# A mixer's values and output gates taken out of its scan, as block products in a stage ahead of it

## The chip, the cores and the metric

The kernel runs on one core of a Trainium2 chip. The metric is the time of one execution on the device in microseconds (us). Its engines are PE (matrix products), DVE (vector), ACT (scalar and function tables), POOL (general) and SP, which here only issues transfers (DMAs) between DRAM and the on-chip memory.

## The reference

One layer: an HGRN2 mixer over 2048 latent tokens of width 1024, behind 256 context tokens, then a gated convolutional feed-forward part (FFN). In short (cut, and for one direction d of two):

```python
q, zf_fwd, zf_bwd, v, g = jnp.split(h @ w_in, 5, axis=-1)        # 8 heads of 128 each
f = lb[d] + (1.0 - lb[d]) * sigmoid(zf)                          # k = 1 - f, q = silu(q)
o_l, _ = hgrn2_chunk_scan(q, k, v, log(f), state_of_context)     # forward and backward, summed
y = (rmsnorm(o_l, g_gain) * silu(g)) @ w_out
lat = lat + g1 * y
lat = lat + g2 * conv_ffn(modulate(rmsnorm(lat), sh2, sc2))
out = rmsnorm(lat, final_g)
```

h is the normalized and modulated input. The vectors g1, sh2, sc2, g2 come from w_ada and the condition.

## The kernel before

Tokens lie in 16 tiles of 128; four tiles are a *unit* (512 tokens), two units a half: g=0 is tiles 0 to 7, g=1 tiles 8 to 15. Every large product is made from three: each fp32 operand is split into a high and a low part (`split`: ACT copies the high part, line 79, DVE subtracts, line 80), and PE adds high x high, high x low and low x high. So a projection of one head and one type for one unit is 8 k-steps of 3 matmuls, 24 of 128x512 (`step`, lines 470 to 472).

`mixer_scan` goes through 16 heads: g=0 with h=0..7, then g=1 with h=0..7. In each it projects two gates (types 2, 1), the query (0), the value (3) and the output gate (4) for the two units of its half. In g=0 it also does gates and value of the context (128x256). The weights of a type are loaded raw (`load_w`, 512 KB) and split in both passes. Values come out transposed and are turned back by PE (line 638). All the small work of the scan (the running products of the gates on DVE, lines 546 and 585, `kd`, `qi`, `km`, `qm`, the `scores` of 32x32 blocks at line 673, masks at 689, their sum `at` at 690, states, outputs at 725 and 728) is placed between the projections by an agenda: each k-step is one *tick*, and `at(clock + n, f)` runs f that many ticks later. Engines work through their instructions in the order in which this program text issues them.

The tokens of the first half are made in the first head (`unit_tok`), those of the second in heads 2 to 5 of g=0 (`make_tok`, `put_tok`, by way of DRAM). The rest of the modulation (`ada_rest`, 32 DVE steps at line 785 and four small products) runs in heads 0 to 5 of g=1, the weighting of the output weights (`out_scaled`, line 812) in heads 2 to 5. Results go to DRAM (`stash`). The FFN already makes its up-projection in 2x2 blocks by seven products (lines 1113 to 1116): the weights of two column blocks and two halves of K are A11, A12, A21, A22, the tokens of two units B11, B12, B21, B22, and sums of them (S1 to S4 of weights, T1 to T4 of tokens) give four results from seven products instead of eight.

Of the kernel before, what the change touches and what calls it, by code (L numbers as in the profile page):

```python
# [11 lines left out]
F32 = mybir.dt.float32  # L12
# [33 lines left out]
def body(ctx, tc, a, out):  # L46
# [104 lines left out]
    Sf = hp.tile([128, NH, 128], F32, name="Sf", tag="Sf", bufs=1)  # L151
    Sb = hp.tile([128, NH, 128], F32, name="Sb", tag="Sb", bufs=1)


    lp = pool_(ch, "lp")
    c1 = ctx.enter_context(ExitStack())
    wp = pool_(c1, "wp", 4)
    hq = pool_(c1, "hq")
    fix = pool_(c1, "fix")
    gp = pool_(c1, "gp", 2)  # L160
    xp = pool_(c1, "xp")
# [4 lines left out]
    TOK = [128, UT, 2, 4, 128]  # L166
    tok = {}
    tok_d = [[dr.tile(TOK, F32, name=f"tok{u}{kh}") for kh in range(2)] for u in range(2)]
    cxt = hq.tile([128, 2, 2, 2, 4, 128], F32R, name="cxt", tag="cxt", bufs=1)
# [6 lines left out]
    def put_tok(hm, t, kh):  # L176

        b = lp.tile([128, 2, 4, 128], F32R, name="stg", tag="stg", bufs=1)
        split(b[:, 0], b[:, 1], hm[:, 4 * kh:4 * kh + 4])
        sp.dma_start(tok_d[t // UT - 2][kh][:, t % UT], b.bitcast(F32))  # L180

    def x_tile(xt, t):
        src, r = (a["x"], t) if t >= 0 else (a["ctx"], t + 2)
        sp.dma_start(xt, src[r * 128:(r + 1) * 128])

    def load_w(h, ty):
        raw = rawp.tile([128, D], F32, name="raw", tag="raw")
        sp.dma_start(raw, a["w_in"][h, ty])
        w = wp.tile([128, 2, KT, 128], F32R, name="w", tag="w")
        split(w[:, 0], w[:, 1], raw.rearrange("p (k n) -> p k n", k=KT))  # L190
        return w

    def new_hm():
        return xp.tile([128, KT, 128], F32, name="hm", tag="hm", bufs=1)

    def load_x(xt, t, hm, *after):
        x_tile(xt, t)
        normalize(xt, hm.rearrange("p k n -> p (k n)"), gp, after)


    HEAD0 = (2, 1, 3, 0)
    staged = {}

    def stage(t):

        tag = ("ke", "ke", "qp", "qp", "qi", "qi", "xt", "hm", "stg", "raw")[t + 2]
        p = {"xt": xp, "hm": xp, "stg": lp, "raw": rawp}.get(tag, gp)
        staged[t] = p.tile([128, D], F32, name="x0", tag=tag, bufs=1 if p in (xp, lp) else 2)
        x_tile(staged[t], t)

    def turn_tok(tp, ts, ks):

        for i, k in enumerate(ks):
            for j, t in enumerate(ts):
                pe.transpose(tp[:, i, j], staged[t][:, k * 128:(k + 1) * 128], ident)
# [6 lines left out]
    with ExitStack() as c0:  # L222
        p0s = pool_(c0, "p0s", space=PSUM)
        silv = sil.rearrange("p (two k) -> p k two", two=2)
        silp = gp.tile([128, KT, 32], F32, name="silp", tag="kt", bufs=2)
# [5 lines left out]
        junk = lp.tile([128, D], F32, name="junk", tag="stg", bufs=1)  # L231
# [5 lines left out]
        def raw_w(ty):  # L237
            raw = rawp.tile([128, D], F32, name="raw", tag="raw")
            sp.dma_start(raw, a["w_in"][0, ty])
            return raw  # L240

        head0 = {}

        def split_head0(ty, raw):
            head0[ty] = w = wp.tile([128, 2, KT, 128], F32R, name="w", tag="w")
            return split(w[:, 0], w[:, 1], raw.rearrange("p (k n) -> p k n", k=KT))
# [10 lines left out]
        head_raw = {}  # L257
        for k in range(2, KT):
            ada_load(act, k, 0)
            ada_load(act if k >= KT - 2 else sp, k, 1)  # L260
            if k == KT - 3:
                head_raw[2] = raw_w(2)
        head_raw[1] = raw_w(1)
        for t in range(4):
            stage(t)
        for t in (-2, -1):
            norm_begin(staged[t], junk, gp)
        norm_end()
        late_junk = place(2, [128, D], F32, "junk")
# [6 lines left out]
        with tc.issue_after(squared[-1]):  # L276
            made = split_head0(2, head_raw[2])
        m2 = gp.tile([128, 512], F32, name="m2", tag="q", bufs=2)
# [15 lines left out]
        hmc = [gp.tile([128, 2, 2, 128], F32, name="hm", tag="gv"[g % 2], bufs=2) for g in range(4)]  # L294
# [4 lines left out]
        def split_ctx(g):  # L299
# [4 lines left out]
        order = [(evict_ctx, 1), (split_ctx, 0), (evict_ctx, 2), (split_ctx, 1), (split_head0, 1),  # L304
                 (evict_ctx, 3), (split_ctx, 2), (split_ctx, 3)]
        for f, g in order:
            with behind_of(made):
                made = f(g, head_raw[1]) if f is split_head0 else f(g)
        head_raw[3] = raw_w(3)
        head_raw[0] = raw_w(0)  # L310
        for t in range(4, 8):
            stage(t)
        with behind_of(made):
            for t in range(4):
                norm_begin(staged[t], late_junk, gp)
                if t == 1:
                    split_head0(3, head_raw[3])
            norm_end()


        l0, l1 = vec[:, V_LB:V_LB + 16], vec[:, V_LB + 16:V_LB + 32]
        lbw = gp.tile([128, 2, 128], F32, name="lbw", tag="so", bufs=2)
# [83 lines left out]

    def mixer_scan():
# [29 lines left out]
        Fs = [fix.tile([128, 2, NS, SEG], F32, name=f"F{i}") for i in range(2)]  # L437
        ABs = [fix.tile([128, UT, 128], F32, name=f"AB{d}") for d in range(2)]
        TBs = [fix.tile([128, 4, UT, 4], F32, name=f"TB{i}") for i in range(2)]
        TXs = [fix.tile([128, 2, UT, 4], F32, name=f"TX{i}") for i in range(2)]  # L440
        for i in range(2):
            pool.memset(Fs[i], 1.0)
            pool.memset(TBs[i], 1.0)
            pool.memset(TXs[i], 1.0)
            pool.memset(ABs[i], 0.0)


        clock = [0]
        agenda = []

        def at(when, f):
            heapq.heappush(agenda, (when, len(asked), f))
            asked.append(when)

        asked = []

        def run(until):
            while agenda and agenda[0][0] <= until:
                heapq.heappop(agenda)[2]()

        def tick():
            clock[0] += 1
            run(clock[0])

        stepped_pe = []

        def step(z, w, r, k):

            h, l = r[:, :, 0, k % 4], r[:, :, 1, k % 4]
            pe.matmul(z, w[:, 0, k], h, start=k == 0, stop=False, skip_group_check=True)  # L470
            pe.matmul(z, w[:, 0, k], l, start=False, stop=False, skip_group_check=True)  # L471
            stepped_pe[:] = [pe.matmul(z, w[:, 1, k], h, start=False, stop=k == KT - 1,  # L472
                                       skip_group_check=True).ins]
            tick()

        def acc(z, w, rs):

            for k in range(KT):
                step(z, w, rs[k // 4], k)
# [7 lines left out]
        evicted = {}  # L487

        def make_tok(t):

            got = []

            def load():
                got.append(xp.tile([128, D], F32, name="xt", tag="xt", bufs=1))
                got.append(new_hm())
                load_x(got[0], t, got[1], *((evicted["kt"], passed[-1]) if t % 2
# [1434 lines left out]
```

## Time and profile before

| | |
|---|---|
| three runs | 2728.62, 2728.97, 2731.67 us; median 2728.97 |
| span of the profiled execution | 2729.5 us (all that is shown of its time) |
| TensorE busy | 2698.7 us, 99% |
| VectorE, ScalarE, GpSimd busy | 1977.8, 1136.9, 572.9 us |
| mean DMA rate | 150 GB/s |

Busy time is the time in which an engine worked on something; with overlapping matmuls the mean length of one is longer than the step from one to the next. The window rows shown below have one stretch of time each, with busy time and count of each engine, then the granted clock of PE, the share of the DMA engines and the rate.

### The profile page before, as it was taken

The page shows a single profiled execution, that of the slowest core. Times are in us where ns is not written, and L with a number is a line of the kernel's source. Part 1 is how long each engine was busy: PE and PEld are TensorE (multiplying, and loading weights), DVE is VectorE, ACT ScalarE, POOL GpSimd, SP SyncE. Part 2 cuts the span into 40 slices and gives each one's busy share as a digit, 9 for nine tenths or more (in the row PEclk, how much of TensorE's full clock was granted, in tenths as well). Part 3 has the DMA queues.
Part 4 walks back from the last instruction along what each step waited for, and adds up shares of the span by engine and source line. Part 5 has one row for each costly group of instructions (what it writes and reads, how often), then busy time and mean ns, then how long its engine had stood idle before and what let it go on. Part 6 is the DMA issues. An engine that isn't in the chain of part 4 may idle for free.

```text
span 2729.5 us, 41987 instructions
## 1 busy us (share of the span) xinstructions
PE 2698.7 (99%) x16060; PEld 2252.7 (83%) x16060; DVE 1977.8 (72%) x2803; ACT 1136.9 (42%) x1887; POOL 572.9 (21%) x885
## 2 busy tenths in 40 slices
PE   7999999999999999999999999999999999999999
PEld 4888888888888888888888888888888888888887
DVE  4756655556767776668997888777877777578896
ACT  5334444323233233335666444444444444333444
POOL 3211111011111111211211543333434440000001
PEclk8999999999999999999999999999999999999999
DMA  6213323224544443228888232228322234988653
GB/s 240 86 53 105 106 83 97 86 87 163 167 124 137 149 137 113 87 80 297 300 300 344 93 93 82 73 79 307 93 76 79 78 93 137 309 279 289 200 185 131
DMA packets 229104, 410.56 MB, mean 150 GB/s; under 512 B 29604, under 2 KB 137508, under 8 KB 225064
## 3 DMA queue, kind: packets, MB, share of 16 engines
q1 hardware_dynamic: 224152, 398.65, 44.1%
q10 hardware_dynamic: 4752, 9.24, 0.9%
q8 instruction: 126, 2.06, 0.3%
q14 instruction: 74, 0.61, 0.1%
HBM read 293.23 MB, written 114.57 MB: 149 GB/s over the span
## 4 chain that ended last, share of the span: by engine, by line
PE 91%; DMA 3%; DVE 3%; ACT 1%; issue 1%; POOL 1%; SPq 0%; ACTq 0%; POOLq 0%; DVEq 0%
PE z L470 11%; PE z L472 11%; PE z L471 11%; PE y L1744 4%; PE y L1743 4%; PE y L1745 4%; PE zc L1113 3%; PE zc L1116 3%; PE zc L1115 3%; PE zd L1113 3%; PE zd L1115 3%; PE zd L1116 3%; PE za L1116 3%; PE za L1115 3%; PE za L1113 3%; PE kv L703 2%
## 5 line engine op out<-in xcount | busy, mean ns | idle before, releaser
L470 PE MATMUL z<-tok,w 128*128 128x512 f32 x1280 | 516.4, 404 | 0.0
L472 PE MATMUL z<-tok,w 128*128 128x512 f32 x1280 | 501.0, 391 | 0.0
L471 PE MATMUL z<-tok,w 128*128 128x512 f32 x1280 | 500.6, 391 | 0.0
L80 DVE TENSOR_TENSOR w<-raw,w 128x512 fp32r<-128x512 f32 (+1 forms) x258 | 237.2, 922 | 131.7 <-ACT w L79 127.8
L472 PEld LDWEIGHTS z<-tok,w 128*128 128x128 f32 x1280 | 240.4, 188 | 52.1
L470 PEld LDWEIGHTS z<-tok,w 128*128 128x128 f32 x1280 | 240.8, 188 | 45.7 <-issue 1.7
L471 PEld LDWEIGHTS z<-tok,w 128*128 128x128 f32 x1280 | 241.1, 188 | 43.9 <-DVE tok L80 0.2
L79 ACT ACTIVATE w<-raw 128x512 fp32r<-128x512 f32 (+1 forms) x258 | 194.8, 760 | 132.9 <-PE zd L1116 75.9
L1743 PE MATMUL y<-w,mh 128*128 128x512 f32 x600 | 233.4, 390 | 1.2 <-ACT X L1777 1.2
L1744 PE MATMUL y<-w,mh 128*128 128x512 f32 x600 | 233.6, 389 | 0.2 <-DVE w L80 0.2
L1745 PE MATMUL y<-w,ml 128*128 128x512 f32 x600 | 233.4, 389 | 0.0
L546 DVE TENSOR_TENSOR_SCAN S<-F,d 128x528 f32<-128x528 f32 (+1 forms) x80 | 91.3, 1144 | 119.1 <-ACT F L525 118.9
L80 DVE TENSOR_TENSOR w<-s,w 128x512 fp32r<-128x512 f32 x126 | 121.5, 967 | 57.2 <-ACT w L79 56.3
L75 POOL TENSOR_TENSOR rs<-rs,mhalf 128x1 f32<-128x1 f32 (+3 forms) x53 | 61.9, 1168 | 417.7 <-DVE rs L74 417.7
L79 ACT ACTIVATE w<-s 128x512 fp32r<-128x512 f32 x126 | 78.5, 628 | 150.5 <-POOL s L1181 83.5
L1113 PE MATMUL zc<-rT,w 128*128 128x512 f32 x352 | 137.1, 390 | 0.2 <-DMA rT<-rhs1T 0.2
L1116 PE MATMUL zc<-rT,w 128*128 128x512 f32 x352 | 136.9, 389 | 0.0
L1115 PE MATMUL zc<-rT,w 128*128 128x512 f32 x352 | 136.9, 389 | 0.0
L1743 PEld LDWEIGHTS y<-w,mh 128*128 128x128 f32 x600 | 112.6, 188 | 25.8 <-ACT X L1777 2.1
L1744 PEld LDWEIGHTS y<-w,mh 128*128 128x128 f32 x600 | 112.6, 188 | 23.9 <-DVE w L80 0.6
L1745 PEld LDWEIGHTS y<-w,ml 128*128 128x128 f32 x600 | 112.6, 188 | 23.3
L1116 PE MATMUL za<-rB,w 128*128 128x512 f32 x336 | 130.7, 389 | 0.0
(359 smaller groups left out, 6259.0 us busy)
## 6 DMA issues: line engine op xcount, KB each, us to landing
raw<-in_w_up_dram SPq DMA_DIRECT2D x88, 512.0 KB, 4.0
raw<-in_w_in_dram SPq DMA_DIRECT2D x80, 512.0 KB, 4.0
lr<-m SPq DMA_DIRECT2D x49, 512.0 KB, 5.2
m<-r SPq DMA_DIRECT2D x66, 256.0 KB, 4.3
spare<-in_w_ada_dram SPq DMA_DIRECT2D x32, 512.0 KB, 4.2
kq<-stash SPq DMA_DIRECT2D x15, 1024.0 KB, 8.0
og<-stash SPq DMA_DIRECT2D x30, 512.0 KB, 5.3
u<-in_w_down_dram SPq DMA_DIRECT2D x51, 256.0 KB, 3.5
```

The lines of the kernel that those rows point to most:

```text
L79: i = act.activation(h, src, AF.Copy)
L80: j = dve.tensor_tensor(l, src, h.bitcast(F32), OP.subtract)
L470: pe.matmul(z, w[:, 0, k], h, start=k == 0, stop=False, skip_group_check=True)
L471: pe.matmul(z, w[:, 0, k], l, start=False, stop=False, skip_group_check=True)
L472: stepped_pe[:] = [pe.matmul(z, w[:, 1, k], h, start=False, stop=k == KT - 1, skip_group_check=True).ins]
L546: dve.tensor_tensor_scan(flat(S[:, d]), flat(F[:, d]), flat(d1[:, 0:ns]), 0.0, OP.mult, OP.max)
L1113: pe.matmul(o, w[:, 0, k], r[:, :, 0, k], start=start and k == 0, stop=False, skip_group_check=True)
L1115: pe.matmul(o, w[:, 0, k], r[:, :, 1, k], start=False, stop=False, skip_group_check=True)
L1116: i = pe.matmul(o, w[:, 1, k], r[:, :, 0, k], start=False, stop=k == 3, skip_group_check=True)
L1743: pe.matmul(z, lh, rh, start=start, stop=False, skip_group_check=True)
L1744: pe.matmul(z, lh, rl, start=False, stop=False, skip_group_check=True)
L1745: pe.matmul(z, ll, rh, start=False, stop=stop, skip_group_check=True)
```

## The change

A stage `early()` stands ahead of the scan and makes all values, and the output gates of all heads in g=0 and of heads 0 to 5 in g=1. A `Heads` object is two heads of one type. With the tokens of the two units of a half they form the 2x2 blocks, and `product` runs one of the seven products, 4 k-steps of 3 matmuls. 105 products (15 pairs) stand in a list `todo`, and weights are prepared `LOOK` = 5 products ahead: raw load, sums S1 to S4 on POOL, splits on ACT and DVE. First come context values (`context_row`) while the tokens of g=1 are made (`unit0`, `unit1`, `differences`), then 7 pairs of g=1, then 8 pairs of g=0. During the first of these, `side_tokens` makes the factors of g=0, one tile of each unit at a time in four rounds, and sends them to DRAM (`tok_d`). When a product is the last of g=1 to use a factor, the factor's place is loaded with that of g=0 (2 MB). `ada_rest` now runs beside the g=0 products. Results are written by `finished`: gates after Silu to the stash, values after the turn (line 475) to `v_d`, context values to `cv_d`.

The scan keeps gates and queries. It loads v, splits weights in g=0 alone and stores them split (`w_d`, 1 MB each), to be loaded ready in g=1. `scores` and the three steps behind them stand 18, 20, 24 and 28 ticks behind a query's end; before they were 16 ticks behind the query, and 5, 9 and 13 behind the value of that unit. The output gates of heads 6 and 7 in g=1 stay plain, at the end of the last head. The context gates have F, TB and TX buffers of their own.

Core of the diff (the list of products, one product, the scan's head):

```diff
+        def multiply(z, w, r, start):
+            for k in range(4):
+                h, l = r[:, :, 0, k], r[:, :, 1, k]
+                pe.matmul(z, w[:, 0, k], h, ...)
+                pe.matmul(z, w[:, 0, k], l, ...)
+                pe.matmul(z, w[:, 1, k], h, ...)
+                tick()
...
+        for i in (0, 2):
+            todo += [(1, p, n) for n in ("B11", "B21") for p in vs[i:i + 2]]
+        for i in (0, 2):
+            todo += [(1, p, n) for n in FACTORS[2:] for p in vs[i:i + 2]]
+        gs = [Heads(4, h) for h in range(0, G_PLAIN, 2)]
+        todo += [(1, p, n) for n in FACTORS for p in gs[0:2]]
+        todo += [(1, gs[2], n) for n in ("B11", "T2", "B21", "T1", "T3", "B22", "T4")]
...
+            product(g, p, n)
+            if last_use[g, n] == i:
+                if g == 1:
+                    rhs[n] = factor_tile(n)
+                    sp.dma_start(rhs[n].bitcast(F32), tok_d[0][n])
...
             def query(u, after):
-                q = swish(project(weight(0), u), "q")
-                done = (made_tok[-1][1],) if first and u == 0 else ()
-                scores, made[u] = unit_steps(h, t0[u], factors(h, u, t0[u], q, done))
-                at(clock[0] + after, scores)
+                q = swish(project(weight(g, h, 0), u), "q")
+                v = values(v_d[h][t0[u] // UT])
+                for f, dt in zip(unit_steps(h, t0[u], factors(h, u, t0[u], q), v), after):
                     at(clock[0] + dt, f)
...
             gate(0)
-            query(0, 16)
+            query(0, (18, 20, 24, 28))
             gate(1)
...
-            value(0, (4, 7, 10) if last else (5, 9, 13))
...
-            out_gate(0)
-                value(1, (5, 9, 13))
-            out_gate(1)
```

ACT's order in the prologue, ahead of the first full products. Before, it is the split of context (`cxt`) and of weights, squares of the first unit (L107, for the norm) and the first gates:

```order
L79 ACTIVATE cxt_149<-hm_280 128x2x256
L107 ACTIVATE junk_213,ss_312<-x0_193 128x1024
L79 ACTIVATE w_323<-raw_300 128x1024
L107 ACTIVATE junk_213,ss_317<-x0_195 128x1024
L107 ACTIVATE junk_213,ss_326<-x0_197 128x1024
L107 ACTIVATE junk_213,ss_332<-x0_199 128x1024
L523 ACTIVATE F1_373<-z_390 128x8x32
L525 ACTIVATE F1_373<-F1_373,lb_111,oml_112 128x8x32
L523 ACTIVATE F1_373<-z_417 128x8x32
```

Now, from the first context values (L502) on, with squares of unit 1 (L129), the turned values (L476) and the weights of the third value pair (`w_541`, `w_544`):

```order
L502 ACTIVATE out_473<-zc_424 128x512
L129 ACTIVATE x0_229,ss_738<-x0_231 128x1024
L129 ACTIVATE x0_229,ss_744<-x0_231 128x1024
L476 ACTIVATE out_473<-tr_498 128x512
L129 ACTIVATE x0_229,ss_750<-x0_231 128x1024
L129 ACTIVATE x0_229,ss_756<-x0_231 128x1024
L502 ACTIVATE out_535<-zc_479 128x512
L476 ACTIVATE out_535<-tr_579 128x512
L79 ACTIVATE w_541<-raw_475 128x512
L79 ACTIVATE w_544<-raw_475 128x512
L79 ACTIVATE aside_384<-raw_477 128x512
```

The splits of that pair's weights stand behind four squares and the results of two context products.

SP's queue where the tokens of the next half come in. Before, that is at the end of g=0 (`tok`, four loads of 2 MB), between the scan's stores:

```order
L715 DMA stash_71<-qi 128x128
L1036 DMA tok<-tok_145 128x4096
L714 DMA stash_64<-sk 128x128
L714 DMA stash_65<-sk 128x128
L1036 DMA tok<-tok_146 128x4096
L748 DMA stash_64<-g 128x128
L748 DMA stash_65<-g 128x128
L748 DMA stash_66<-g 128x128
```

Now it is the turn from g=1 to g=0 in the new stage, with the factors `rB11`, `rT2`, `rB21`, `rT1` and the raw weights of the second value pair of g=0:

```order
L524 DMA stash11_75<-out_2173 128x128
L737 DMA rB11_2199<-tok0B11_131 128x4096
L737 DMA rT2_2218<-tok0T2_133 128x4096
L524 DMA stash8_72<-out_2241 128x128
L524 DMA stash9_73<-out_2241 128x128
L524 DMA stash10_74<-out_2241 128x128
L524 DMA stash11_75<-out_2241 128x128
L737 DMA rB21_2247<-tok0B21_132 128x4096
L583 DMA raw_1233<-in_w_in_dram 128x1024
L583 DMA raw_1233<-in_w_in_dram 128x1024
L737 DMA rT1_2273<-tok0T1_134 128x4096
```

Three of the 2 MB loads stand ahead of the two raw weights.

DVE in a head of g=1, from the next unit's scans to this unit's `at` (S and F are the running products, AB the masked scores, `spare` the weighted output weights). Before:

```order
L80 TENSOR_TENSOR w<-raw,w 128x1024
L546 SCALAR_TENSOR_TENSOR S<-F_373,d_369 128x528
L553 TENSOR_TENSOR ke<-S 128x512
L585 SCALAR_TENSOR_TENSOR F_373<-F_373,d_369 128x528
L546 SCALAR_TENSOR_TENSOR S<-F_373,d_369 128x528
L689 COPY_PREDICATED AB_374<-mb,sc_365 128x512
L689 COPY_PREDICATED AB_375<-mf,sc_366 128x512
L554 TENSOR_TENSOR ke<-S 128x16x32
L690 TENSOR_TENSOR at<-AB_374,AB_375 128x512
L785 SCALAR_TENSOR_TENSOR acc<-spare,sil,acc 128x1024
L585 SCALAR_TENSOR_TENSOR F_373<-F_373,d_369 128x528
```

Now:

```order
L938 TENSOR_TENSOR ke<-S 128x512
L970 SCALAR_TENSOR_TENSOR F_3697<-F_3697,d_3693 128x528
L931 SCALAR_TENSOR_TENSOR S<-F_3697,d_3693 128x528
L939 TENSOR_TENSOR ke<-S 128x16x32
L970 SCALAR_TENSOR_TENSOR F_3697<-F_3697,d_3693 128x528
L972 RECIPROCAL rt<-S 128x32
L957 TENSOR_TENSOR km<-ke,TX_3705 128x4x64
L1066 COPY_PREDICATED AB_3699<-mb,sc_3689 128x512
L1066 COPY_PREDICATED AB_3700<-mf,sc_3690 128x512
L957 TENSOR_TENSOR km<-ke,TX_3705 128x4x64
L1067 TENSOR_TENSOR at<-AB_3699,AB_3700 128x512
L1155 SCALAR_TENSOR_TENSOR spare<-spare,vec,g_9148 128x1024
L1083 SCALAR_TENSOR_TENSOR states<-Sf,sd,kv 128x128
```

The masks of a unit stand behind both scans of the next unit's second gate, its `rt` and half of its `km`; before they stood between them, and the projections of value and output gate lay behind the scores.

More of the change, by code (lines that the diff above doesn't have):

```diff
@@ L309, in body @@
[L309 to L317, printed above, removed]
-            norm_end()
+                made = f(g)
+        sp.dma_start(cxt_d, cxt.bitcast(F32))
+        p0.close()
+        ps = pool_(ce, "pse", 2, space=PSUM)
+        aside = place(2, [128, 4, 2, 4, 128], F32R, "aside")
@@ new lines, in early, with __init__, prepare @@
+        class Heads(Blocks):
+            def __init__(self, ty, h):
+                super().__init__(ring)
+                self.ty, self.h, self.z, self.loaded = ty, h, {}, False
+            def prepare(self, n):
+                if LEFT[n] in self.w:
+                    return
+                if not self.loaded:
+                    self.loaded = True
+                    self.raws([raw_tile() for _ in range(2)])
+                    for i, r in enumerate(self.raw):
+                        sp.dma_start(r.rearrange("p i k n -> p (i k n)"), a["w_in"][self.h + i, self.ty])
+                    self.sums(pool, *[pb.tile([128, 4, 128], F32, name=n, tag=n) for n in ("s1", "s2")])
+                self.split(LEFT[n])
@@ L739, in second @@
                 stepped(1)
-            return scores, (vs.append, lambda: stepped(0), second, lambda: outputs(1))
+            return scores, lambda: stepped(0), second, lambda: outputs(1)
         def keep_gate(h, t0, g):
```

810 lines of the change are left out of this document (506 added, 304 removed).

## The prediction

> **What bounds the kernel now.** I read the page's sums by engine and by chain first, then its costliest group, the time line of that group, and a table of windows by stage.
>
> ```profile
> span 2729.5 us, 41987 instructions
> PE 2698.7 (99%) x16060; PEld 2252.7 (83%) x16060; DVE 1977.8 (72%) x2803; ACT 1136.9 (42%) x1887; POOL 572.9 (21%) x885
> PE 91%; DMA 3%; DVE 3%; ACT 1%; issue 1%; POOL 1%; SPq 0%; ACTq 0%; POOLq 0%; DVEq 0%
> L470 PE MATMUL z<-tok,w 128*128 128x512 f32 x1280 | 516.4, 404 | 0.0
> ```
>
> PE is busy 99% of the span and carries 91% of the chain. L470 is one of three equal lines (L470, L471, L472), so the scan's projections are 3840 matmuls of 128x512. Their mean of 404 ns counts the overlap of one with the next; the time line has the real step:
>
> ```profile
> 567.73 0.39 PE L470 MATMUL z<-tok,w 128*128 128x512 f32 x1
> ...
> 574.99 0.39 PE L472 MATMUL z<-tok,w 128*128 128x512 f32 x1
> ```
>
> These are 33 rows, 32 steps in 7.26 us: 0.2269 us a matmul, each behind the last.
>
> ```profile
> core 0: us, PE busy (x) PEld busy (x) DVE busy (x) ACT busy (x) POOL busy (x), PEclk, DMA share, GB/s
> 0.00:35.00 35.00, 17.80 (x85) 4.22 (x85) 6.90 (x24) 7.82 (x13) 13.84 (x33) 0.90 0.96 378
> 35.00:102.00 67.00, 64.31 (x441) 54.51 (x442) 57.58 (x93) 41.99 (x72) 20.34 (x39) 0.95 0.21 75
> ...
> 557.00:635.00 78.00, 78.00 (x609) 67.36 (x608) 44.62 (x66) 24.11 (x42) 11.63 (x31) 1.00 0.29 89
> 635.00:702.50 67.50, 67.50 (x522) 57.16 (x521) 41.50 (x58) 20.25 (x34) 10.26 (x24) 1.00 0.62 210
> 702.50:772.00 69.50, 69.50 (x526) 57.26 (x525) 47.88 (x66) 21.28 (x36) 10.26 (x24) 1.00 0.38 117
> 1600.00:1700.00 100.00, 100.00 (x442) 82.78 (x442) 80.48 (x91) 48.34 (x67) 34.90 (x42) 1.00 0.24 74
> ```
>
> The rows are the load of the start, the prologue, a head of the first pass (g=0), two heads of the second (g=1; the last with the modulation's remainder), and a piece of the FFN. From 557 on PE is full in each, and DVE is next at 57 to 69% of a head. The FFN row matters as a model: that stage already runs the seven-product scheme, and there PE is full with DVE at 80%. In this kernel a matmul taken out of a full window is time taken out, as long as the others keep up.
>
> **The matmuls removed.** Values and output gates of 15 head pairs (four value pairs in both halves of the tokens, four gate pairs in one, three in the other) cost 15 x 2 heads x 2 units x 24 = 1440 matmuls before, and 15 x 7 products x 12 = 1260 after. Gates of heads 6 and 7 in the second half stay plain. 180 fewer x 0.2269 = **40.8 us off PE**. Context values, transposes of tokens and of values are as many as before, only elsewhere. Everything below says how much of 40.8 the other engines let through.
>
> **The prologue: +6.** Before, PE's loss up to 102 us is the idle of the window's row, 67.00 - 64.31 = 2.7 us, and a slow stretch:
>
> ```profile
> 34.33 0.39 PE L470 MATMUL z<-cxt,w 128*128 128x256 f32 x1 [1.05 <-ACT cxt L79]
> ...
> 39.16 0.41 PE L470 MATMUL z<-cxt,w 128*128 128x256 f32 x1
> ...
> 43.21 0.41 PE L471 MATMUL z<-cxt,w 128*128 128x256 f32 x1
> ...
> 44.60 0.28 PE L472 MATMUL z<-cxt,w 128*128 128x256 f32 x1
> 44.72 0.29 PE L470 MATMUL z<-cxt,w 128*128 128x256 f32 x1
> ```
>
> From 39.16 to 43.21 there are 19 steps of 0.213 us where later ones take 0.12, so 1.8 us more: about 5 in all. Now ACT must prepare both later units of tokens and five sets of factors before the third kind of product (T2) can run. By the order of the changed kernel these are its rows 14 to 111: 53 splits of 128x512, 20 copies, 8 modulations of 512 and four of 256, 10 squares. Durations from the same work in the window 35 to 102:
>
> ```profile
> L79 ACT ACTIVATE tok<-hm 128x512 fp32r<-128x512 f32 x16 | 9.8, 629 | 3.2 <-DVE hm L220 3.0
> L107 ACT ACTIVATE junk<-x 128x1024 f32<-128x1024 f32 x8 | 8.4, 1047 | 0.1
> L219 ACT ACTIVATE hm<-tp,B,A 128x512 f32<-128x512 f32 x8 | 6.2, 775 | 2.4 <-PE tp L215 2.1 <-DVE tok L80 0.3
> ...
> L107 ACT ACTIVATION_READ_ACCUMULATOR junk<-x 128x1 f32 x8 | 1.5, 185 | 0.0
> L639 ACT ACTIVATE v<-tr 128x512 f32<-128x512 f32 x1 | 0.6, 602 | 1.2 <-PE tr L638 1.2
> ...
> L219 ACT ACTIVATE hm<-tp,B,A 128x256 f32<-128x256 f32 x1 | 0.6, 553 | 0.0
> ```
>
> That is 53 x 0.63 + 20 x 0.6 + 8 x 0.775 + 4 x 0.55 + 10 x 1.24 = 66 us. PE has meanwhile 192 context matmuls of 0.12 (23), 96 of 128x512 for the first eight products (21.8), 24 for T2 (5.4) and some 100 transposes of about 0.09, together 59 us. ACT can begin at about 28 us and is done near 94 if it never waits; PE, from 34.3, near 93. But each waits for the other, and ACT's queue is in order: the splits of the third value pair now stand behind the squares of unit 1, which wait for their tokens. I take 11 us of loss for PE, 6 more than before. Ends: 0 (they overlap as well as before) and +18, where unit 1's share of ACT (24 splits and 4 modulations, 15.1 + 3.1) lies wholly bare.
>
> The slow stretch stands in the granted clock too (0.95 in the window's row), and came behind waits of 1 us and less. The Trainium skill, "TensorE: Matmul & The Clock Gate", Part 1, has the clock fall to half only after an idle window of about 3.4 us and return after as much work. The trace agrees on the half (0.213 against 0.12) and not on the length of the wait. By that rule a bare wait of 4 us in one of the new stages would cost about 1.7 us more, and the sum below would be 2710 instead of 2708.
>
> **New stage, second half of the tokens (g=1): +2.** ACT's rows 112 to 243 are 72 splits, 60 modulations of 128x128, 22 copies and Silus and 6 squares. A small modulation is one of these:
>
> ```profile
> L142 ACT ACTIVATE hm<-tp,B,A 128x128 f32<-128x128 f32 x156 | 57.1, 468 | 16.2 <-PE tp L138 16.0
> ```
>
> All of it makes 95 us, beside some 41 products and the transposes, 118 us of PE. ACT is then at 80%, far over its 48 in the FFN row but below PE. DVE and POOL do what they do in the FFN row, with weights split five products (13.6 us) ahead. Ends: 0, and +10, one product (2.7) bare for each of the four side tiles that are prepared here.
>
> **Turn-over from g=1 to g=0: +4.** The factors are replaced in their places by 2 MB loads, and on SP's queue those of B11, T2 and B21 stand ahead of the raw weights of the second value pair.
>
> ```profile
> raw<-in_w_in_dram SPq DMA_DIRECT2D x80, 512.0 KB, 4.0
> ...
> tok<-tok SPq DMA_DIRECT2D x4, 2048.0 KB, 9.2
> ```
>
> B21's place is free when the 45th product ends, and the raw weights are needed for the 51st: five products, 13.6 us. At the 378 GB/s of the first window's row T2 and B21 take 11.1, two raw tiles 2.8, landing and split about 3: 17, so 3.4 of wait; I take 4. Ends: 0 (the transfers share the engines) and +10 (one 9.2 load wholly bare).
>
> **The g=0 part and the border to the scan: +2.** This part has no tokens to make and takes over the modulation's 32 DVE steps, hidden as in the row 702.50, where PE stays full beside them. At the border POOL writes the scan's constants, the first gate weights are split, and ACT changes its table, 1.3 us by this row:
>
> ```profile
> 1.74 1.28 ACT L254 ACT_TABLE_LOAD   x1 [1.74 <-PEq L1922]
> ```
>
> By the order these weights are loaded early and their splits stand before the last products' sums, so little is bare. Ends: 0, and +8, one load of 4.0 with a split of 2.3 and the table.
>
> **The scan: +5, and +1 in its last head.** A unit has 72 projection matmuls instead of 120. A g=0 head falls from 78.0 by 96 x 0.2269, the context values' 24 x 0.12 and the turns of v (about 1.4), to 52 us; a g=1 head from 67.5 by 21.8 and 1.2 to 44.5. DVE must fit into that:
>
> ```profile
> L80 DVE TENSOR_TENSOR w<-raw,w 128x1024 fp32r<-128x1024 f32 x5 | 6.1, 1220 | 7.1 <-ACT w L79 6.9 <-PE o L728 0.3
> L546 DVE TENSOR_TENSOR_SCAN S<-F,d 128x528 f32<-128x528 f32 x4 | 5.0, 1256 | 9.5 <-ACT F L525 9.5
> L585 DVE TENSOR_TENSOR_SCAN F<-F,d 128x528 f32<-128x528 f32 x4 | 5.0, 1249 | 0.0
> L785 DVE SCALAR_TENSOR_TENSOR acc<-spare,sil,acc 128x1024 f32<-128x1024 f32 x2 | 2.6, 1276 | 0.0
> ...
> L531 DVE TENSOR_TENSOR g<-z,g 128x512 f32<-128x512 f32 x2 | 1.4, 687 | 1.9 <-ACT g L530 1.9
> ```
>
> In g=1 the splits (6.1), the modulation (2.6 and 0.7) and the gates (1.4) go: 41.5 - 10.8 = 31 of 44.5, 69%, and 75% in heads 2 to 5 with two output-weight steps of 1.28. In g=0 two of the splits and the gates go: 44.6 - 3.8 = 41 of 52, 78%. The FFN row has PE full at 80%, but what counts here is order: on DVE the next unit's second pair of scans now stands ahead of the masks that PE's outputs wait for. The same place before:
>
> ```profile
> 707.28 0.36 PE L673 MATMUL sc<-qp,ke 128*32 128x32 f32 x16
> ...
> 708.23 1.23 DVE L546 TENSOR_TENSOR_SCAN S<-F,d 128x528 f32<-128x528 f32 x1
> 709.38 0.72 DVE L689 COPY_PREDICATED AB<-mb,sc 128x512 f32<-128x512 uint32 x1
> ...
> 711.26 0.70 DVE L690 TENSOR_TENSOR at<-AB,AB 128x512 f32<-128x512 f32 x1
> ...
> 728.87 0.38 PE L725 MATMUL o<-Sf,qi 128*128 128x128 f32 x2
> ```
>
> From the scores' end (707.64) to the end of at are 4.3 us, with one scan in them. The outputs that read it followed only at 728.87, 21 us behind the scores, so this was never felt:
>
> ```profile
> PE y L1247 <- DVE wo L80: 0.4, 1, 0.4
> ```
>
> (the only wait of PE from 162 to 1240 us). Now they follow after 18 projection matmuls. From the start of the scores PE has 1.3 of scores, 0.7 of transposes, 6 and 12 projection matmuls (4.1) and about 0.9 of state products: 7.0 us. DVE has, from about the same moment (the second gate ends six matmuls, 1.4 us, earlier, and ACT's two steps take as long), L546 and L585 (2.5) with ke, a reciprocal and km (1.4, estimated as one full and two half tiles beside the 0.7 of L531), masks (1.3), km (0.4), at (0.7): 6.3. About 0.7 us of room, and 3 to 4 us of slack in a unit of 22. I take a slip of 0.6 in the eight units where an output-weight step (1.28) also stands ahead of the states: 5 us. Ends: 0, and the third rival below. The last head's four plain gates are the same matmuls as before in another place: +1, ends 0 and +3.
>
> **Sum.** 2729.5 - 40.8 + 6 + 2 + 4 + 2 + 5 + 1 = 2708.7 for the profiled execution, whose span is all that is shown of it; the median of the runs is 0.5 lower, so 2708.
>
> **Rivals.** (1) Everything is hidden: only 2 of the prologue stays, 2729.5 - 40.8 + 2 = 2691. The FFN row speaks for it, ACT's 66 us against PE's 59 in the prologue against it. (2) ACT becomes the bound in the new stage: both of its terms at their ends, 2729.5 - 40.8 + 18 + 10 + 4 + 2 + 5 + 1 = 2729, no change. For it speak the 80% there and an in-order queue that also waits for POOL's sums; against it, that the FFN does as much beside a full PE. (3) Slower: the scan turns from PE's pace to that of the chain scores, masks, at, outputs. If the scans ahead come one pair later (2.5 us) than I place them, each unit is late by 2.5 less the room of 0.7 and 0.3 of other slip, 1.5 us. In 32 units that is 48: 2729.5 - 40.8 + 15 + 48 = 2752. It decides from 0.81 us a unit on, (40.8 - 15) / 32. For it speaks the fall from 21 us to 7; against it, that DVE has 3 to 4 us of slack in each unit to catch up. That the products would not be 180 fewer is excluded by the order, which has 1260 of them and 2400 plain ones.
>
> **How the numbers follow.** The forecast's own case 0.53 (2699 to 2718, its terms about half way to their ends), everything hidden 0.18, ACT bound 0.16, scan late 0.13. Faster by over 0.2% (5.5 us, about what a measurement of this kernel can tell) hold the first two and 0.05 of the third: 0.76. The same, 0.11, is the rest of the third; slower, 0.13, is the last. The range runs from rival 1 to just past rival 2, 2690 to 2735, and leaves out the late scan.
>
> **What would show it.** In the changed kernel PE's sum near 2655 to 2665 us, by 41 lower, and waits of PE on ACT between 45 and 95 us totalling 5 to 10. One wait of some 4 us on DMA near the turn-over (about 95 + 118 us). Heads at 52 and 45 us in the scan, with waits of PE on DVE at the outputs of 0.3 us or less a unit; 1 us and more there would be rival 3. The prediction is wrong if the prologue's waits pass 20 us, or if heads of g=1 take over 47.

## The result, and the profile after

The changed kernel takes 2763.64 us (median; 2760.85 to 2765.10), the kernel before 2729.83 beside it: a ratio of 1.0125, 95% interval 1.0113 to 1.0137. It is 34 us slower where 21 less were forecast. Forecast (2708) and result lie 56 us apart, and the profile says where most of it lies. First the page of the changed kernel, to be read against the four lines of before:

```profile
span 2763.4 us, 42399 instructions
PE 2677.8 (97%) x15880; PEld 2226.0 (81%) x15880; DVE 2079.7 (75%) x2941; ACT 1163.1 (42%) x1987; POOL 684.8 (25%) x956
```

PE has exactly 180 instructions fewer (15880 for 16060), so the matmuls did go. But it is busy 97% instead of 99%, and its busy time fell by 21 us only, where 180 matmuls are 40.8. (The page follows the chain back over less than half of the span here, so it is not used.) The windows by stage, before and after, with the columns of the prediction:

```profile
35.00:135.00 100.00, 97.19 (x733) 83.79 (x734) 74.44 (x119) 52.97 (x92) 20.34 (x39) 0.97 0.28 90
135.00:1230.00 1095.00, 1094.90 (x8445) 928.74 (x8444) 702.95 (x1028) 375.12 (x654) 173.08 (x423) 1.00 0.35 111
```

```profile
35.00:135.00 100.00, 79.18 (x444) 65.92 (x445) 72.80 (x100) 66.67 (x123) 35.73 (x29) 0.88 0.61 225
135.00:235.00 100.00, 95.67 (x466) 77.75 (x465) 76.93 (x114) 68.56 (x143) 33.25 (x26) 1.00 0.76 281
235.00:275.00 40.00, 31.77 (x129) 25.38 (x129) 19.19 (x29) 13.25 (x24) 14.09 (x7) 0.87 0.94 366
275.00:440.00 165.00, 158.43 (x706) 124.00 (x705) 110.57 (x123) 57.24 (x96) 45.40 (x39) 1.00 0.71 248
440.00:851.40 411.40, 408.92 (x3664) 355.37 (x3663) 308.32 (x474) 135.01 (x240) 99.38 (x256) 1.00 0.47 160
851.40:1184.00 332.60, 319.00 (x2922) 270.86 (x2922) 241.08 (x366) 85.25 (x162) 73.01 (x170) 1.00 0.44 148
1184.00:1262.00 78.00, 76.08 (x676) 64.69 (x676) 53.34 (x89) 27.83 (x60) 12.34 (x29) 1.00 0.31 95
```

The rows after the change are the prologue, most of the g=1 products, the turn-over, the g=0 products, and the scan's eight heads of g=0, first seven of g=1, and last head. Before, from 35 us up to the output product at 1230, PE idled 2.9 us. After, it idled 20.8 in the prologue, 4.3 while the g=1 products and the side tokens run, 8.2 at the turn-over, 6.6 in the g=0 products, and 2.5, 13.6 and 1.9 in the three parts of the scan: 58 us. The granted clock adds to it, 0.88 over 79 us of work and 0.87 over 32 (some 13 us if the shortfall is taken as lost, 3 before). The two together are 55 + 11 = 66 more, against 40.8 saved: 25 of the 32 us by which the output product starts later (1262 against 1230). The remaining 7 lie where PE counts as busy; no run here places them.

In the scan, a head of g=0 repeats every 52.2 us by its first projection, as costed (52). The first seven heads of g=1 go from 851.5 to 1184.1, 47.5 us each (46.6 to 48.3) where 44.5 were forecast; 1.9 of the 3.0 more is PE's idle time. So the loss is for the larger part ahead of the scan, and in one wait within it.

**The prologue.** On the time lines of PE, ACT, DVE and POOL, 98 to 130 us:

```profile
98.56 0.39 PE L514 MATMUL za<-tok,w 128*128 128x512 f32 x1
101.35 0.66 PE L475 MATMUL tr<-ident,out 128*128 128x128 f32 x4 [2.39 <-ACT hm L240]
...
124.97 0.79 PE L511 MATMUL za<-rT,w 128*128 128x512 f32 x1 [3.96 <-ACT w L79]
```

```profile
98.99 1.15 ACT L79 ACTIVATE rT<-hm 128x512 fp32r<-128x512 f32 x2 [2.12 <-PE za L514]
...
124.28 1.67 ACT L79 ACTIVATE w<-s 128x512 fp32r<-128x512 f32 x3 [2.91 <-POOL s L213]
```

```profile
113.28 0.68 DVE L80 TENSOR_TENSOR w<-s,w 128x512 fp32r<-128x512 f32 x1
113.88 1.76 DVE L80 TENSOR_TENSOR tok<-hm,tok 128x512 fp32r<-128x512 f32 x1
...
121.83 0.67 DVE L543 TENSOR_TENSOR u<-u,za 128x512 f32<-128x512 f32 x1
```

```profile
113.50 1.59 POOL L451 TENSOR_TENSOR hm<-hm 128x512 f32<-128x512 f32 x1 [2.02 <-ACT tok L79]
...
121.43 1.60 POOL L218 TENSOR_TENSOR raw<-raw 128x512 f32<-128x512 f32 x1
```

At 98.8 PE has used up the products that need no differences, and until 125 it gets scraps. ACT stood at 98.99 in front of a split into `rT2` until PE had read the last weights that lie in the same place. Then come modulation, differences and splits, each waiting for the one before on another engine, and the first weights for T2 wait for POOL's sums. DVE's split of one and the same size takes 0.68 us or 1.76. The long one begins inside a POOL addition and ends 0.55 us behind its end (115.64 and 115.09). The third row, as large but with one input in PSUM (`za`), lies wholly beside a POOL addition and takes 0.67.

**The turn-over.** SP's queue, ACT and PE:

```profile
243.62 0.38 SPq L737 DMA_DIRECT2D rB<-tok0B  x1
244.09 0.38 SPq L737 DMA_DIRECT2D rT<-tok0T  x1
...
246.75 0.42 SPq L737 DMA_DIRECT2D rB<-tok0B  x1
247.27 4.57 SPq L583 DMA_DIRECT2D raw<-in_w_in_dram  x2
```

```profile
263.95 1.67 ACT L79 ACTIVATE w<-raw 128x512 fp32r<-128x512 f32 x3 [6.69 <-DMA raw<-in_w_in_dram]
```

```profile
264.63 0.80 PE L511 MATMUL za<-rB,w 128*128 128x512 f32 x1 [8.00 <-ACT w L79]
...
268.64 0.63 PE L511 MATMUL za<-rB,w 128*128 128x512 f32 x1
```

The raw weights are issued behind three 2 MB loads, and the first of them lands 16.6 us later; PE waits 8.0 us, and its next ten steps take 0.44 us on average instead of 0.227. B11's load, the first of the three, is issued at 243.62, although the last product that reads its place ends at 236.9: SP issues stores until then. So it falls together with T2's and B21's. The DMA engines are full meanwhile (362 to 437 GB/s in slices of 4 us from 248 to 264).

**The third pair of g=0** (queue of SP, then PE):

```profile
282.66 0.38 SPq L477 DMA_DIRECT2D v<-out  x1
297.18 0.33 SPq L689 DMA_DIRECT2D spare<-in_w_ada_dram  x1
...
300.20 0.99 SPq L583 DMA_DIRECT2D raw<-in_w_in_dram  x2
```

```profile
308.39 0.50 PE L511 MATMUL za<-rB,w 128*128 128x512 f32 x1 [3.04 <-ACT w L79]
```

SP stands still for 14 us in front of a modulation load whose place DVE has not read yet, and the raw weights stand behind it.

**In the scan** PE's longest sum of waits is this one, 15 of the 16 in g=1 and the other just ahead of its first projection:

```profile
PE kv L1080 <- ACT sk L1086: 13.5, 16, 1.1
```

The time lines of DVE, ACT and PE in a unit of head 3:

```profile
1011.37 0.68 DVE L1067 TENSOR_TENSOR at<-AB,AB 128x512 f32<-128x512 f32 x1
...
1013.17 0.34 DVE L1083 SCALAR_TENSOR_TENSOR states<-Sf,sd,kv 128x128 f32<-128x128 f32 x1
```

```profile
1014.98 0.38 ACT L1086 ACTIVATE sk<-kv 128x256 f32<-128x256 f32 x1 [6.16 <-DVE states L1083]
```

```profile
1015.42 1.16 PE L1080 MATMUL kv<-v,kt 128*128 128x128 f32 x8 [1.15 <-ACT sk L1086]
```

There is one `kv` tile in PSUM. The second group of state products waits until ACT has copied the first group out, and ACT does so after DVE's first states. These stand on DVE's queue behind masks, `at` and, in heads 2 to 5, an output-weight step. DVE is busy almost without a gap from 1006 to 1015 us there.

### The profile page after: what moved, and what is told of

It reads as the page before. It is cut to its first block, busy times and chain, and to the rows that moved or that the text cites. A ratio compares the mean times of both kernels' runs of the same rounds, so it can differ in the third digit from the quotient of the medians.

```text
span 2763.4 us, 42399 instructions
## 1 busy us (share of the span) xinstructions
PE 2677.8 (97%) x15880; PEld 2226.0 (81%) x15880; DVE 2079.7 (75%) x2941; ACT 1163.1 (42%) x1987; POOL 684.8 (25%) x956
## 5 line engine op out<-in xcount | busy, mean ns | idle before, releaser
L80 DVE TENSOR_TENSOR w<-raw,w 128x512 fp32r<-128x512 f32 (+1 forms) x262 | 219.5, 843 | 79.7 <-ACT w L79 68.6
L79 ACT ACTIVATE w<-raw 128x512 fp32r<-128x512 f32 (+1 forms) x262 | 174.1, 671 | 180.9 <-PE zd L1404 75.0
L80 DVE TENSOR_TENSOR w<-s,w 128x512 fp32r<-128x512 f32 x171 | 163.3, 960 | 71.8 <-ACT w L79 70.4
L887 PE MATMUL z<-tok,w 128*128 128x512 f32 x512 | 206.8, 404 | 0.0
L889 PE MATMUL z<-tok,w 128*128 128x512 f32 x512 | 200.2, 391 | 0.0
L888 PE MATMUL z<-tok,w 128*128 128x512 f32 x512 | 199.7, 390 | 0.0
L79 ACT ACTIVATE w<-s 128x512 fp32r<-128x512 f32 x171 | 106.4, 628 | 174.6 <-POOL s L213 97.2
L212 POOL TENSOR_TENSOR s<-raw 128x512 f32<-128x512 f32 x57 | 99.8, 1751 | 247.1 <-DMA raw<-in_w_up_dram 127.0
L911 ACT ACTIVATE F<-z 128x512 f32<-128x512 f32 (+1 forms) x80 | 44.4, 555 | 216.0 <-PE z L889 216.0
L75 POOL TENSOR_TENSOR rs<-rs,mhalf 128x1 f32<-128x1 f32 (+3 forms) x53 | 55.0, 1040 | 313.6 <-DVE rs L74 313.6
L1403 PE MATMUL za<-rB,w 128*128 128x512 f32 x336 | 130.7, 389 | 0.0
L1404 PE MATMUL za<-rB,w 128*128 128x512 f32 x336 | 130.7, 389 | 0.0
```

The lines of the kernel that those rows point to most:

```text
L79: i = act.activation(h, src, AF.Copy)
L80: j = dve.tensor_tensor(l, src, h.bitcast(F32), OP.subtract)
L212: eng.tensor_tensor(s1, a21, a22, OP.add)
L889: pe.matmul(z, w[:, 1, k], h, start=False, stop=k == KT - 1, skip_group_check=True)
L1403: pe.matmul(o, w[:, 0, k], r[:, :, 1, k], start=False, stop=False, skip_group_check=True)
L1404: i = pe.matmul(o, w[:, 1, k], r[:, :, 0, k], start=False, stop=k == 3, skip_group_check=True)
```

## The experiments

Each is the changed kernel with the edit shown, timed against the kernel before on the same chip.

**Spacing in the scan.**

```diff
-            query(0, (18, 20, 24, 28))
+            query(0, (18, 20, 26, 30))
```

> The changed kernel with one edit: the third and fourth step behind a query's scores come 26 and 30 ticks after the query instead of 24 and 28, so the second group of state products has 18 projection matmuls (4.1 us) behind the first instead of 12. Theory (latency): PE waits in the scan only because the one kv tile in PSUM is read by ACT (sk) after DVE's states, 13.5 us in 16 waits in g=1; with 1.4 us more they go, heads of g=1 fall from 45.0 to 44.0 and the time by 12 to 15 us, from 2763.6 to about 2750. Rival (DVE has no room in the shorter heads): the wait only moves to another product, less than 4 us gained.

Measured 2762.39 us, ratio 1.0124 (1.0109 to 1.0139): 1 us. The wait for sk is gone, and the g=1 part shrank by 7 us, not by 12 to 15 (its first projection moved from 851.5 to 853.9, the output product from 1262.0 to 1257.7; the 45.0 us a head that the theory starts from are 47.5 by the first projections). But another wait stands in its place, in g=0, where the context's states now collide with it, and the g=0 part grew by 2.5 us:

```profile
PE kv L1080 <- DVE Sf L1030: 5.6, 7, 0.8
PE o L1101 <- DVE states L1083: 2.5, 9, 0.4
```

The theory has the wait right for g=1, the rival holds for g=0. In the kernels below that combine edits with this one, the spacing is 24 and 28 in g=0, 26 and 30 in g=1.

**Raw weights early.** They are asked for when the pair that held their place has its last split issued:

```diff
                 p_.prepare(n_)
                 ready += 1
+                if n_ == "T4":
+                    q = pairs.index(p_) + 2
+                    if 4 <= q < len(pairs):
+                        pairs[q].load()
```

> The changed kernel with one edit: the raw weights of a pair are asked for as soon as the pair that used their place has had its last split issued, instead of with the pair's first product. At the turn-over they then stand ahead of two of the 2 MB factor loads. Theory (queue order): the 8.0 us wait for w at 264.6 us falls to under 2, the slow clock after it goes too, and the 3.0 at 308 shrinks: 8 to 13 us less, about 2753. Rival (transfer rate: 6 MB of factors and 1 MB of weights must come in any case): the wait reappears at the first product with a reloaded factor, 0 to 4 us gained.

Measured 2763.52 us, 1.0129 (1.0114 to 1.0144): nothing. As the rival has it, the wait for w gave way to one for the factor itself:

```profile
PE za L511 <- DMA rB<-tok0B: 5.1, 1, 5.1
```

The 2.9 us between 8.0 and 5.1 do not arrive either: the wait for the modulation's sums (`acc`) at 311 us grows from 0.8 to 3.8.

**The first eight products in another order** (third and fourth pair first):

```diff
-        for i in (0, 2):
+        for i in (2, 0):
             todo += [(1, p, n) for n in ("B11", "B21") for p in vs[i:i + 2]]
```

> The changed kernel with one edit: of the first eight products those of the third and fourth value pair come first. Their weights lie in the place that T2's factor takes, so that place is free about 10 us earlier and ACT no longer waits at 98.99 us for PE's last use of it with the rest of the tokens' work behind. Theory (a shared place stops ACT's queue): the hole of PE from 98.8 to 125 us shrinks by 8 to 12 us, time about 2753. Rival (the chain transposes, modulation, differences, splits of unit 1 is simply that long): less than 3 us gained.

Measured 2764.40 us, 1.0131 (1.0114 to 1.0148): nothing. But the windows show a gain that is given back:

```profile
35.00:135.00 100.00, 83.52 (x479) 69.93 (x480) 80.19 (x113) 71.00 (x132) 37.73 (x30) 0.95 0.66 243
135.00:235.00 100.00, 92.88 (x437) 76.23 (x436) 70.01 (x105) 67.00 (x137) 30.96 (x25) 0.95 0.74 267
```

The prologue's idle time falls from 20.8 to 16.5 and its clock rises from 0.88 to 0.95; the next 100 us lose 7.1 instead of 4.3 and their clock falls to 0.95. So the shared place was worth about half of what the theory had, and not even that reaches the end.

**Sums of weights on DVE.**

```diff
-                    self.sums(pool, *[pb.tile(...) ...])
+                    self.sums(dve, *[pb.tile(...) ...])
```

(and sum3, sum4 of these pairs likewise.)

> The changed kernel with one edit: the sums of weights in the new stage (four per pair, 128x512) are made by DVE instead of POOL. Theory (latency and places): they are not what PE waits for in most places, 5 us less to 5 more. Rival (DVE's splits take 1.2 to 1.8 us instead of 0.69 while POOL works beside them, and this holds up the factors): splits return to 0.69 and the time falls by 10 to 20 us, although DVE gets 57 sums of 0.7 us more.

Measured 2751.79 us, 1.0086 (1.0071 to 1.0101): 12 us less. The scan starts at 427 instead of 440. DVE's splits from 35 to 240 us, in the changed kernel and in this one:

```profile
L80 DVE TENSOR_TENSOR w<-s,w 128x512 fp32r<-128x512 f32 x21 | 17.9, 864 | 8.1 <-ACT w L79 8.1
L80 DVE TENSOR_TENSOR rT<-hm,rT 128x512 fp32r<-128x512 f32 x16 | 16.0, 1017 | 6.8 <-ACT rT L79 6.1
```

```profile
L80 DVE TENSOR_TENSOR w<-s,w 128x512 fp32r<-128x512 f32 x21 | 14.0, 682 | 0.0
L80 DVE TENSOR_TENSOR rT<-hm,rT 128x512 fp32r<-128x512 f32 x16 | 11.3, 731 | 7.3 <-ACT rT L79 6.9
```

The rival was right about the time and the splits. Whether the gain lies in the splits or in the sums coming sooner was still open, so one more kernel leaves the sums on DVE and gives POOL additions whose results are not used:

```diff
+            if n in ("S1", "S2", "S3", "S4") and self.eng is dve:
+                x = self.src[n]
+                for i in range(2):
+                    pool.tensor_tensor(scratch[0], x[:, 2 * i:2 * i + 2], x[:, 2 - 2 * i:4 - 2 * i], OP.add)
```

> As the kernel with the sums of weights on DVE (alone -12 us), but POOL makes for each sum two additions of 128x256 that read the same weights and whose results are not used. Theory (POOL beside DVE slows DVE's splits): the splits rise again from 0.68 to 0.8 to 1.0 us in the mean and more than half of the 12 us is lost, 2758 to 2766. Rival (the sums came late because POOL takes 1.6 us for what DVE does in 0.69, and waits its turn behind other POOL work): the time stays near 2752, 2748 to 2755.

Measured 2775.59 us, 1.0175 (1.0158 to 1.0192): all of the 12 us is lost, and 12 more, beyond the range of the theory. The rows of DVE's splits and of POOL's additions:

```profile
L80 DVE TENSOR_TENSOR w<-s,w 128x512 fp32r<-128x512 f32 x20 | 19.4, 986 | 0.0
```

```profile
L236 POOL TENSOR_TENSOR scratch<-s 128x256 f32<-128x256 f32 x40 | 41.6, 1040 | 30.9 <-DVE s L213 26.3 <-DVE s L223 2.1
```

POOL's work costs time although nobody reads it. It loads POOL with more than the original sums did (168.6 us from 35 to 455, 131.1 in the changed kernel), and a place of weights also stays held until POOL has read it, so the size is no clean price of the contention; the direction is clear. Sums that come late cannot be the reason for the slow splits here, as DVE makes the sums.

**Three edits together.** Sums on DVE, the other order of the first products, the spacing in g=1:

> Three edits together: sums of weights on DVE (alone -12 us), the first eight products with the third and fourth pair first (alone 0, since what it won before 135 us was lost again by 195), and the later spacing of the scan's last two steps in g=1 alone (in both passes it gave 9 us in g=1 and took 5 in g=0). Theory (POOL's sums slow DVE's splits and hold the side tokens, so that they ate the swap's gain): the three add up, -12 - 6 - 9: about 2737. Rival (they share one cause and do not add): 2742 or more, with the loss between 135 and 195 us again at 10 or more.

Measured 2734.54 us, 1.0020 (1.0010 to 1.0030): 29 us less, where one by one they gave 12, 0 and 1 (the spacing in both passes). They add up as the theory has it. The scan starts 20 us earlier, at 420 (at 427 with the sums on DVE alone), and its g=1 part takes 398.9 us instead of 410.5. The stretch from 135 to 235, which took the swap's gain back beside POOL's sums, now loses 0.5 us:

```profile
135.00:235.00 100.00, 99.51 (x479) 81.07 (x478) 77.22 (x135) 67.85 (x139) 9.87 (x8) 1.00 0.80 294
```

**The order of loads at the turn-over.** Early raw weights and T2's factor behind B21's:

```diff
-                if g == 1:
-                    rhs[n] = factor_tile(n)
-                    sp.dma_start(rhs[n].bitcast(F32), tok_d[0][n])
+                if g == 1 and n != "T2":
+                    for m in (n, "T2") if n == "B21" else (n,):
+                        rhs[m] = factor_tile(m)
+                        sp.dma_start(rhs[m].bitcast(F32), tok_d[0][m])
```

> The early raw loads (alone 0: the wait of 8.0 us for w became one of 5.1 for the reloaded B11) and T2's reload put behind B21's, which is needed two products earlier. Theory (order of transfers): B11 and the raw weights no longer share the engines with T2, the wait falls below 2 us, time about 2759. Rival (the 8 MB that must pass there in 16 us at about 400 GB/s set the time): the wait only moves to the products of B21 or T2, time 2762 or more.

> Early raw loads and T2's reload behind B21's, without the second load of B12 that the earlier version of this edit made (2 MB in the same stretch). Theory (order of transfers): B11 lands before it is needed, the wait at the turn falls below 2 us, about 2757. Rival (rate): B11 still lands some 13 us or more behind its issue, wait 3 to 5 us, about 2763.

The first also loaded B12 in that stretch, 2 MB that nothing needed there: 2765.02 us, 1.0128 (1.0113 to 1.0143), no gain. Without it: 2756.89 us, 1.0102 (1.0088 to 1.0115), 7 us less. In the first the wait for B11 was 4.9 us, in the second, from 235 to 440 us:

```profile
PE za L511 <- ACT w L79: 3.0, 2, 1.6
...
PE za L511 <- DMA rB<-tok0B: 0.9, 1, 0.9
```

So both theories hold in part: with 2 MB more the wait stays, and with only what is needed, in order of need, that for B11 falls to 0.9 us.

**The modulation later.**

```diff
-                    at(clock[0] + 2 + 6 * m, lambda: next(rest, None))
+                    at(clock[0] + 60 + 4 * m, lambda: next(rest, None))
```

> As the one before, and the modulation's remainder begins 58 ticks (40 us) later beside the g=0 products and runs denser. Theory (SP's queue: raw weights of the third and fourth g=0 pair stood behind modulation loads that waited for DVE): the loss between 295 and 335 us, 9 to 11 us, falls to 4 or less, another 5 to 7 us. Rival (the place of the raw weights is not free earlier): the loss stays.

> The changed kernel with the modulation's remainder beginning 58 ticks later and denser, nothing else. Theory (SP's queue behind modulation loads): the 3.0 us wait at 308 and what follows go, 7 to 10 us less, about 2755. Rival (it took early raw loads to win the 9.5 us): 0 to 3 us.

With the first order of loads, the second load of B12 in it: 2755.51 us, 1.0093 (1.0078 to 1.0108), 9.5 less than that order alone. By itself: 2756.22, 1.0096 (1.0081 to 1.0112), 7 less than the changed kernel. Of PE's waits from 235 to 440 us one is left, the turn-over:

```profile
PE za L511 <- ACT w L79: 8.4, 1, 8.4
```

So the modulation's early place was the cause of what was lost at 308 us and after. That it worked by SP's queue is read from the time line: the raw weights are issued at 284.3 us instead of 300.2. The edit also moves the modulation's steps on DVE, and no run separates the two.

**All together.**

> All of these edits together: early raw loads, T2 behind B21, modulation late, sums on DVE, the swap, the spacing in g=1. If the losses are separate places, the sum is -12 - 6 - 9 - 4 - 6: about 2727, as fast as the kernel before. If the new stage is bound by the transfers or by DVE as such, 2735 or more.

Measured 2729.07 us, 0.9998 (0.9988 to 1.0007). In this kernel the list of pairs followed the new order of the first products, so early loads put weights into places of other pairs: the same amount of work with weights exchanged, so its time can be compared though its output is not the layer's. It also had the second load of B12. With the list in the order of use, B12 once, and the differences of unit 1 on DVE as well:

> The edits of the combined kernel, with the early raw loads in the order of the pairs' use and B12 loaded once, and the differences of unit 1 on DVE as well. Theory (separate places, each with its own queue): turn-over and modulation give another 8 to 10 us over the three edits' 2734.5, the differences 2 to 3: about 2722 to 2726, below the kernel before. Rival (transfers bind the turn-over): 2729 as the combined kernel showed.

Measured 2718.00 us, 0.9957 (0.9945 to 0.9970): 12 us faster than the kernel before, 46 faster than the changed one, and 4 below the range of the theory. The differences on DVE were not run alone. The windows of this kernel up to the scan, which starts at 404:

```profile
35.00:135.00 100.00, 90.77 (x524) 76.91 (x525) 84.16 (x143) 74.47 (x141) 6.47 (x10) 0.97 0.77 286
135.00:235.00 100.00, 97.67 (x470) 79.60 (x469) 74.34 (x129) 65.67 (x136) 10.11 (x8) 1.00 0.78 284
235.00:275.00 40.00, 38.98 (x184) 31.91 (x182) 18.40 (x29) 13.51 (x24) 0.00 (x0) 1.00 0.99 407
275.00:404.00 129.00, 129.00 (x571) 100.60 (x570) 99.34 (x131) 50.84 (x85) 5.04 (x16) 1.00 0.75 256
```

Of 40 us of idle time in the new stage 12.6 are left, 9.2 of them in the prologue. Against the kernel before, 12 of the 40.8 us taken off PE arrive. DVE does the sums too and is busy 84% of the prologue and less elsewhere.

## Why the prediction was wrong, point by point

- *The matmuls removed, 40.8 us.* Right: 180 instructions fewer.
- *The prologue, +6.* The step that failed worst. It weighed sums, 66 us of ACT beside 59 of PE, and took overlap for most. ACT was busy 66.7 of 100 us, so its sum was right and did not set the time. The first two products with T2, by the sums done some 104 us from the start (93, and 11 of loss), were done at 129.9. PE idled 20.8 us against 2.8 before, 18 more, which was the upper end and past the prediction's own sign of being wrong (20), and the slow clock came on top (0.88 against 0.97). What set the time is a chain from engine to engine. Two of its links were tested: the shared place in ACT's way (20.8 to 16.5 us of idle time without it) and splits slowed by POOL (20.8 to 16.4). All edits together leave 9.2; what these hang on was not tested.
- *The g=1 products, +2.* The sentence that DVE and POOL do what they do in the FFN was the missing term. It was true, and it hides that splits beside POOL take longer: in the FFN's window from 1600 to 1700 before, the splits of weight sums already took 1.01 us in the mean, with PE full. That DVE has weights far enough ahead there, while here factors and weights were on the path, is a reading and not tested. Moving POOL's sums gave 12 us, spread over the whole stage: idle time fell from 20.8 to 16.4 in the prologue, from 4.3 to 1.8 here, from 6.6 to 3.8 in the g=0 products.
- *The turn-over, +4.* The mechanism was right, raw weights behind factors, the size too small: 8.2 us idle, and 2.1 of slow clock (ten steps of 0.2 more) behind it. The rate was as costed (378 GB/s; 362 to 437 measured). What was mis-sized is the amount: T2's and B21's 4 MB were counted, and B11's 2 MB, issued 6.7 us after its place was last read, behind stores on SP's queue, passed in the same stretch. At the prediction's own rate they are 5.5 us, by estimate. That the stores delayed it is read from the time line; the runs with other orders show that the order decides.
- *The g=0 part, +2.* Failed in "hidden as in the row 702.50" for the modulation. That row is right for DVE's steps beside a full PE; its loads now stood on SP's queue ahead of raw weights. Beginning it later gave 7 us. The queue that the loads were moved onto was not counted.
- *The scan, +5, and +1.* PE's waits there are 18 us, 12 more than these terms. `at` was in time, as costed. The step that failed is the slip: 0.6 us was taken in the eight units with an output-weight step ahead of the states, and none in the others. Measured are 1.15 in those and 0.6 in the other units of g=1, and they are felt not at the outputs but at the second group of state products, which needs the single `kv` tile back. These groups are 12 matmuls apart before and after. Before, DVE's states came 1.6 us behind the first group (722.88 and 724.51), now 3.8 (1009.42 and 1013.17), behind the masks and `at`. So heads of g=1 took 47.5 us, over the 47 that the prediction named as a sign of being wrong. Half a microsecond of the 3.0 too many is a term of its sum: the turns of v were taken off at 1.2 us a head, their busy time, and two steps of 0.36 are what they cost PE before.
- *The rivals.* Rival 2 had the stage right and the engine wrong; ACT did not bind, DVE at 73 to 77% did not either. Rival 3, the scan late at `at`, did not happen; its kind of chain, scans and masks on DVE ahead of what PE needs, did, with 0.6 to 1.15 us a unit in g=1 alone. Its chance of 0.13 was the only one above the range.

## What to carry to other kernels

When work is taken out of a stage that hid it and put into one of its own, cost the new stage by its chains and not by sums per engine: which product is the last that needs nothing new, what stands ahead of the next one on each in-order queue, and which place must be read first. A queue of transfers is a resource like an engine: a load that waits for a free place stops every load behind it, so what is needed first must be issued first, and nothing unneeded in between. One edit alone can show nothing because the next wait takes its place (two here gave 0 and 1 us), so the windows are to be read before it is dropped: with a third that alone gave 12, and one of them confined to g=1, they gave 29.

## What the runs showed of the hardware

POOL's additions slow DVE's steps. The same 128x512 split took 0.68 us with POOL quiet and up to 1.78 beside a POOL addition, and additions that nobody reads cost 24 us (2751.79 to 2775.59). They read as a wait and not as a lower speed: in the changed kernel, each of the 41 splits of this size from 35 to 440 us that took over 1 us ends 0.55 us behind the end of a POOL addition. Twelve DVE steps of this size with one input in PSUM lie wholly beside POOL additions in the same stretch, and take 0.67 to 0.69. The Trainium skill, "GPSIMD Engine Reference", section 1, Specifications, says that GpSimd shares its SBUF interfaces with VectorE, with contention where an instruction of VectorE has two inputs in SBUF. The traces agree, with 2.6 times as the largest ratio.

A transfer that waits for its place holds those behind it on the queue: 14 us on SP's from 282.66 to 297.18.

After the 8.0 us wait PE's steps were 0.43 us for 4.5 us, and after the single one of 3.04 at 308.39 they were 0.23 to 0.39 and full within three. The rule weighed in the prediction (The Trainium skill, "TensorE: Matmul & The Clock Gate", Part 1: half the clock after an idle window of about 3.4 us) fits both. In the prologue the clock fell to 0.88 in the mean where waits of 2 to 4 us followed each other with little work between.
